# MLP up in a hybrid encoder layer: each matmul as two over half of the contraction, summed by ScalarE and VectorE

## The chip, the cores and the metric

The kernel runs on one core of a Trainium2 chip. The metric is the device time of one execution in microseconds, as the median of several runs. The engines in the text: PE (TensorE) multiplies matrices and writes only to PSUM, an accumulator memory of 8 banks, each of 128 partitions by 512 fp32 values; PEld is its loading of weights; ACT (ScalarE) and DVE (VectorE) work elementwise; POOL is GpSimd; SP issues the DMAs that bring weights from main memory.

## The reference

One layer of an encoder over 512 tokens of 1024 features: a mixer with three branches, a cross-attention into 256 memory tokens, and a gated MLP, each between two RMS norms and with a residual. The change concerns the first half of the MLP:

```
D_MODEL = 1024; SEQ = 512; D_FF = 2816

def dwconv3(x, w):                      # centred, width 3, over the tokens, one filter per channel
    xp = jnp.pad(x, ((0, 0), (1, 1), (0, 0)))
    return xp[:, :-2] * w[0] + xp[:, 1:-1] * w[1] + xp[:, 2:] * w[2]

def conv_glu_ffn(h, w_up, w_conv, w_down):
    u = dwconv3(h @ w_up, w_conv)       # 512 x 5632
    g, val = jnp.split(u, 2, axis=-1)
    return (jax.nn.gelu(g, approximate=True) * val) @ w_down
```

All arrays are fp32.

## The kernel before

**Products in three parts.** Every fp32 operand is split into a high part (what the fp32r format holds; ACT makes it, `high`, line 75) and a low part (the rest; DVE makes it, `low`, line 78). A product is then three fp32r matmuls into one PSUM bank: high × high, high × low, low × high (`mm3`, lines 88 to 90). Weights come by DMA as blocks of 128 × 1024 (`wr`, three buffers), and are split into `wh` and `wl` (four buffers each), so a block's buffers come free when PE has finished the block four before.

**MLP up.** `mlp_up` makes the 5632 columns of `h @ w_up` as 44 blocks of 128 channels by 512 tokens, in the order gate 0, value 0, gate 1, value 1, and so on. A block takes 8 steps over the contraction (1024 = 8 × 128) of 3 matmuls, all into one bank (`mm`, four buffers in turn): the weights are 128 × 128 pieces of `wh` and `wl`, the moving operand is the normed input, `hh` and `hl`, with 512 columns. The first four blocks (`AHEAD`) are made in two halves of 256 tokens each, because the last two of the four token tiles are still being normed; the other 40 are made whole, by `project_all`.

**What follows a block.** `conv3` does the convolution out of PSUM in three steps into an SBUF tile `u`: ACT writes the middle tap (line 322), DVE adds the left tap (323) and the right tap (331), each reading the bank again. Then ACT applies `gelu` to a gate block (line 1021); for a value block DVE multiplies by the gate (1024), ACT makes the high part of the result and DVE the low part (75 and 78, both called `act`), which stay in SBUF for MLP down.

**MLP down.** `mlp_down` takes four `mm` banks, one for each tile of 128 tokens, and accumulates over 22 `act` tiles, twice (for the two halves of the 1024 output columns).

**What sets the order.** A scheduler places the instructions of each engine in one list ahead of time, and on the chip each engine works through its list in order, waiting on semaphores where an operand or a buffer isn't ready. In the middle of MLP up the scheduler puts, for each block n, the splitting of the weights of block n+4 ahead of block n's convolution, on ACT and on DVE. Banks and buffers go round: block n+4 writes the bank of block n. `aux` names a second set of four PSUM banks, used by transposes, attention and sums elsewhere, and by nothing in MLP up before the change.

Of the kernel before, what the change touches and what calls it, by code (L numbers as in the profile page):

```python
# [9 lines left out]
ALU = mybir.AluOpType  # L10
# [3 lines left out]
P = 128  # L14
# [3 lines left out]
KD = D // P  # L18
# [32 lines left out]
class Trunk:  # L51
# [865 lines left out]
    def project_all(self, ps, w, ht):  # L917
        for k in range(KD):
            c = slice(k * P, (k + 1) * P)
            self.mm3(ps[:], tuple(q[:, c] for q in w), tuple(q[:, :, k, :] for q in ht), k == 0, k == KD - 1)  # L920


    def keys(self, kv, mem, tiles):
        km = []
        for kt in tiles:
            ps = self.project(self.d["xa_wk"][kt], mem, M)
            h, lo = (kv.tile([P, M], F32R, tag="km" + q, bufs=KD, name="km") for q in "hl")
            self.split(h[:], lo[:], ps[:, :M])
            km.append((h[:], lo[:]))
        return km  # L930
# [65 lines left out]
    def mlp_up(self, tp, ap, ht, last):  # L996
        nc, d = self.nc, self.d
        order = [i + KF * s for i in range(KF) for s in range(2)]
        pend = []
        for n, c in enumerate(order[: self.AHEAD]):  # L1000
            w = self.block(d["ffn_up"][c])
            ps = self.mm_bank()
            self.project_half(ps, w, ht, 0)
            pend.append((w, ps))
            if n == 1:
                last[0]()
        last[1]()
        act = []
        for n, c in enumerate(order):
            if n < self.AHEAD:  # L1010
                w, ps = pend[n]
                self.project_half(ps, w, ht, 1)
            else:
                w = self.block(d["ffn_up"][c])
                ps = self.mm_bank()
                self.project_all(ps, w, ht)
            val = n % 2
            u = tp.tile([P, L], F32, tag="u%d" % val, bufs=2, name="u")
            self.conv3(u[:], ps[:], [FFW + tap * 44 + c for tap in range(3)])
            if not val:  # L1020
                nc.scalar.activation(out=u[:], in_=u[:], func=ACT.Gelu_apprx_tanh)
                g = u
            else:
                nc.vector.tensor_tensor(out=u[:], in0=u[:], in1=g[:], op=ALU.mult)  # L1024
                h, lo = (ap.tile([P, L], F32R, tag="act" + q, bufs=KF, name="act") for q in "hl")
                self.split(h[:], lo[:], u[:])
                act.append((h, lo))
        return act
# [319 lines left out]
```

## Time and profile before

| | us |
|---|---|
| median of 3 runs | 1096.74 (1094.62 to 1097.0) |
| the profiled execution | 1093.87 |
| its span, first to last instruction | 1092.1 |
| last matmul of the half-made blocks; first of the whole ones | 747.38; 747.50 |
| last matmul of MLP up; first of MLP down | 964.91; 965.13 |
| first matmul of MLP down into its fourth bank | 969.02 |

How to read it: times in the profile are microseconds from the start of the span. A row of the order of time has the start, the duration, the engine, the line of the kernel, the instruction, what it writes and reads by the program's names, and the shapes; in brackets stands how long the engine had been idle and what ended that. A row of the waits has who waited for whom, the sum, the count and the longest. A row of a group has the count, then busy time, mean ns of one, and idle time ahead. A row of a stretch has its length, then busy time (and count) of PE, PEld, DVE, ACT and POOL, and PE's granted clock (1.00 is full).

### The profile page before, as it was taken

To read this page: it belongs to the slowest core of one execution; us is meant where nothing else is said; L and a number is where in the kernel's file an instruction comes from. 1 tells how busy PE (TensorE), PEld (TensorE's weight loads), DVE (VectorE), ACT (ScalarE), POOL (GpSimd) and SP (SyncE) were. 2 spreads that over 40 slices of the span, in tenths; PEclk is the share of its full clock that TensorE was granted. 3 is DMA by queue.
4 is the path that set the end of the run, shared out by engine and by line. 5 is a ranking of instruction groups with operands and counts; after the bars stand their busy time and mean duration, and the time that the engine had idled before them with its cause. 6 is when DMAs were issued, how large, how long until landed. Compare 5 with 4: busy or idle time off the path is not lost.

```text
span 1092.1 us, 13531 instructions
## 1 busy us (share of the span) xinstructions
PE 1071.0 (98%) x5232; PEld 895.3 (82%) x5232; DVE 691.7 (63%) x1037; ACT 476.8 (44%) x744; POOL 66.2 (6%) x56
## 2 busy tenths in 40 slices
PE   8889999999999999999999999999999999999997
PEld 6677888887888888888798888898888888888886
DVE  6898799986665763436795456577565656542324
ACT  6554443326557642324564445345444444431211
POOL 0161120001110100000000000000000000000000
PEclk9889999999999999999999999999999999999999
DMA  6354622326332322226245321133222222222212
GB/s 222 106 192 159 234 100 97 129 84 178 110 117 93 104 78 97 97 96 230 98 151 196 117 77 53 64 98 116 97 97 97 97 97 97 97 97 97 97 58 77
DMA packets 43532, 125.48 MB, mean 115 GB/s; under 512 B 5097, under 2 KB 11561, under 8 KB 43468
## 3 DMA queue, kind: packets, MB, share of 16 engines
q1 hardware_dynamic: 43468, 124.62, 33.5%
q8 instruction: 41, 0.67, 0.2%
q14 instruction: 23, 0.19, 0.0%
HBM read 115.16 MB, written 7.34 MB: 112 GB/s over the span
## 4 chain that ended last, share of the span: by engine, by line
PE 88%; DVE 5%; DMA 4%; ACT 2%; issue 1%; SPq 1%; DVEq 0%; ACTq 0%
PE mm L88 26%; PE mm L89 26%; PE mm L90 26%; PE aux L89 2%; PE aux L88 2%; PE aux L90 2%; DMA wr<-in_w_out 1%; DVE wl L78 1%; DMA wr<-in_w_in 1%; PE aux L725 1%; PE aux L714 1%; PE aux L904 1%; DMA raw<-in_hy_f 1%; ACT wh L75 1%; DMA v<-vd 0%
## 5 line engine op out<-in xcount | busy, mean ns | idle before, releaser
L78 DVE TENSOR_TENSOR wl<-wr,wh 128x1024 fp32r<-128x1024 f32 (+1 forms) x171 | 216.8, 1270 | 250.9 <-ACT wh L75 248.1
L75 ACT ACTIVATE wh<-wr 128x1024 fp32r<-128x1024 f32 (+1 forms) x171 | 180.1, 1054 | 304.1 <-PE mm L89 177.4
L89 PE MATMUL mm<-hl,wh 128*128 128x512 f32 (+1 forms) x448 | 167.5, 374 | 0.0
L88 PE MATMUL mm<-hh,wh 128*128 128x512 f32 (+1 forms) x448 | 167.2, 374 | 0.2 <-ACT hh L75 0.2
L90 PE MATMUL mm<-hh,wl 128*128 128x512 f32 (+1 forms) x448 | 167.4, 374 | 0.0
L88 PE MATMUL mm<-xh,wh 128*128 128x512 f32 x416 | 164.0, 394 | 0.0
L89 PE MATMUL mm<-xl,wh 128*128 128x512 f32 x416 | 163.2, 392 | 0.0
L90 PE MATMUL mm<-xh,wl 128*128 128x512 f32 x416 | 162.6, 391 | 0.0
L90 PEld LDWEIGHTS mm<-hh,wl 128*128 128x128 f32 x448 | 84.3, 188 | 15.0
L88 PEld LDWEIGHTS mm<-hh,wh 128*128 128x128 f32 x448 | 84.1, 188 | 15.3 <-ACT hh L75 0.5
L89 PEld LDWEIGHTS mm<-hl,wh 128*128 128x128 f32 x448 | 84.4, 188 | 15.0 <-DVE hl L78 0.2
L88 PEld LDWEIGHTS mm<-xh,wh 128*128 128x128 f32 x416 | 78.6, 189 | 16.2 <-issue 0.3
L90 PEld LDWEIGHTS mm<-xh,wl 128*128 128x128 f32 x416 | 78.4, 188 | 16.4
L89 PEld LDWEIGHTS mm<-xl,wh 128*128 128x128 f32 x416 | 78.5, 189 | 15.8 <-issue 0.3
L88 PE MATMUL mm<-wh,act 128*128 128x512 f32 x176 | 68.5, 389 | 0.0
L89 PE MATMUL mm<-wl,act 128*128 128x512 f32 x176 | 68.5, 389 | 0.0
L90 PE MATMUL mm<-wh,act 128*128 128x512 f32 x176 | 68.3, 389 | 0.0
L75 ACT ACTIVATE act<-u 128x512 fp32r<-128x512 f32 x22 | 13.9, 631 | 57.8 <-DVE u L1024 57.8
L88 PEld LDWEIGHTS mm<-wh,act 128*128 128x128 f32 x176 | 33.0, 188 | 7.1 <-issue 0.3
L90 PEld LDWEIGHTS mm<-wh,act 128*128 128x128 f32 x176 | 33.0, 188 | 6.9
L89 PEld LDWEIGHTS mm<-wl,act 128*128 128x128 f32 x176 | 33.0, 188 | 6.8
L331 DVE SCALAR_TENSOR_TENSOR u<-mm,cols,u 128x511 f32<-128x511 f32 x44 | 33.1, 751 | 1.5
(338 smaller groups left out, 1895.9 us busy)
## 6 DMA issues: line engine op xcount, KB each, us to landing
wr<-in_w_in SPq DMA_DIRECT2D x55, 512.0 KB, 3.5
wr<-in_ffn_up SPq DMA_DIRECT2D x44, 512.0 KB, 3.5
wr<-in_ffn_down SPq DMA_DIRECT2D x22, 512.0 KB, 3.4
wr<-in_w_branch SPq DMA_DIRECT2D x12, 512.0 KB, 3.4
kd<-kt SPq DMA_DIRECT2D x16, 256.0 KB, 3.8
kst<-kd SPq DMA_DIRECT2D x8, 512.0 KB, 4.9
wr<-in_w_out SPq DMA_DIRECT2D x8, 512.0 KB, 4.0
wr<-in_xa_wk SPq DMA_DIRECT2D x8, 512.0 KB, 3.4
```

What stands on the lines that cost most here:

```text
L75: self.nc.scalar.activation(out=out, in_=in_, func=ACT.Copy, bias=0.0, scale=scale)
L78: (eng or self.nc.vector).tensor_tensor(out=out, in0=in_, in1=f(high), op=ALU.subtract)
L88: mm(out, ah, bh, start=first, stop=False)
L89: mm(out, ah, bl, start=False, stop=False)
L90: mm(out, al, bh, start=False, stop=last)
L331: nc.vector.scalar_tensor_tensor(out=out[:, 0 : L - 1], in0=ps[:, 1:L], scalar=self.colvec(w2), in1=out[:, 0 : L - 1], op0=ALU.mult, op1=A ...
L714: nc.tensor.transpose(tr[:, i * P : (i + 1) * P], s[:, i // 2, (i % 2) * P : (i % 2 + 1) * P], self.ident[:])
L725: self.nc.tensor.matmul(po[64 * e : 64 * e + 64, b * P : (b + 1) * P], v[b, j][:, (h + e) * 64 : (h + e + 1) * 64], pt[:, (2 * i + j) * P ...
L904: self.nc.tensor.transpose(tr[:, k * P : (k + 1) * P], t[:, c : c + P], self.ident[:])
```

## The change

Of the 40 whole blocks, each matmul over 128 rows of the contraction is made as two over 64 rows each: rows 0 to 63 into an `mm` bank, rows 64 to 127 into an `aux` bank, in turns. The two matmuls of a pair use the two halves of the array's rows. After the block, ACT copies the `aux` bank into the tile `u`, DVE adds `u` to the `mm` bank in place, and the convolution reads the `mm` bank as before. The first four blocks stay as they were. Lines after these move by 14 (the multiplication by the gate is at 1038 then, `gelu` at 1035); the new add is line 1032.

```
@@ -919,6 +919,16 @@
+    def project_rows(self, banks, w, ht):
+
+        mm = self.nc.tensor.matmul
+        for k in range(KD):
+            c = slice(k * P, (k + 1) * P)
+            (wh, wl), (xh, xl) = (q[:, c] for q in w), (q[:, :, k, :] for q in ht)
+            for i, (a, b) in enumerate(((wh, xh), (wh, xl), (wl, xh))):
+                for ps, r in zip(banks, (slice(0, 64), slice(64, P))):
+                    mm(ps[:], a[r], b[r], start=k == i == 0, stop=k == KD - 1 and i == 2)
@@ -1012,10 +1022,14 @@
             else:
                 w = self.block(d["ffn_up"][c])
-                ps = self.mm_bank()
-                self.project_all(ps, w, ht)
+                banks = self.mm_bank(), self.aux_bank()
+                self.project_rows(banks, w, ht)
+                ps, other = banks
             val = n % 2
             u = tp.tile([P, L], F32, tag="u%d" % val, bufs=2, name="u")
+            if n >= self.AHEAD:
+                self.high(u[:], other[:])
+                nc.vector.tensor_tensor(out=ps[:], in0=ps[:], in1=u[:], op=ALU.add)
             self.conv3(u[:], ps[:], [FFW + tap * 44 + c for tap in range(3)])
```

The order on ACT for a pair of blocks late in MLP up, before (`wh` is the split of the block four later, `u_…<-mm_…` the middle tap, the third row `gelu`):

```order
L75 ACTIVATE wh_8184<-wr_8186 128x1024
L322 ACTIVATE u_8063<-mm_8038,cols_176 128x512
L1021 ACTIVATE u_8063<-u_8063 128x512
L75 ACTIVATE wh_8220<-wr_8222 128x1024
L322 ACTIVATE u_8099<-mm_8074,cols_176 128x512
L75 ACTIVATE act_8104<-u_8099 128x512
L75 ACTIVATE wh_8283<-wr_8285 128x1024
```

and the same place on ACT after the change:

```order
L75 ACTIVATE wh_9210<-wr_9212 128x1024
L75 ACTIVATE u_9006<-aux_8957 128x512
L322 ACTIVATE u_9006<-mm_8956,cols_176 128x512
L1035 ACTIVATE u_9006<-u_9006 128x512
L75 ACTIVATE wh_9273<-wr_9275 128x1024
L75 ACTIVATE u_9069<-aux_9020 128x512
L322 ACTIVATE u_9069<-mm_9019,cols_176 128x512
L75 ACTIVATE act_9076<-u_9069 128x512
L75 ACTIVATE wh_9363<-wr_9365 128x1024
```

The copy of the `aux` bank has come between the split of the weights and the middle tap; the rest keeps its place. On DVE, the same pair of blocks before:

```order
L78 TENSOR_TENSOR wl_8221<-wr_8222,wh_8220 128x1024
L323 SCALAR_TENSOR_TENSOR u_8099<-mm_8074,cols_176,u_8099 128x511
L331 SCALAR_TENSOR_TENSOR u_8099<-mm_8074,cols_176,u_8099 128x511
L1024 TENSOR_TENSOR u_8099<-u_8099,u_8063 128x512
L78 TENSOR_TENSOR act_8105<-u_8099,act_8104 128x512
L78 TENSOR_TENSOR wl_8284<-wr_8285,wh_8283 128x1024
```

and after:

```order
L78 TENSOR_TENSOR wl_9274<-wr_9275,wh_9273 128x1024
L1032 TENSOR_TENSOR mm_9019<-mm_9019,u_9069 128x512
L323 SCALAR_TENSOR_TENSOR u_9069<-mm_9019,cols_176,u_9069 128x511
L331 SCALAR_TENSOR_TENSOR u_9069<-mm_9019,cols_176,u_9069 128x511
L1038 TENSOR_TENSOR u_9069<-u_9069,u_9006 128x512
L78 TENSOR_TENSOR act_9077<-u_9069,act_9076 128x512
L78 TENSOR_TENSOR wl_9364<-wr_9365,wh_9363 128x1024
```

The add stands behind the split of the weights and ahead of the two side taps. On PE, where MLP down begins, the scheduler puts off the fourth bank (the one that the last block of MLP up has used) while it fills the first three. Before, 17 matmuls stand ahead of the first row of this piece that writes `mm_8282`:

```order
L89 MATMUL mm_8281<-wl_8284,act_6736 128x512
L88 MATMUL mm_8282<-wh_8283,act_6674 128x512
L89 MATMUL mm_8282<-wl_8284,act_6674 128x512
L90 MATMUL mm_8282<-wh_8283,act_6675 128x512
L90 MATMUL mm_8281<-wh_8283,act_6737 128x512
```

and 22 ahead of the first that writes `mm_9362` now:

```order
L90 MATMUL mm_9359<-wh_9393,act_6867 128x512
L88 MATMUL mm_9360<-wh_9393,act_6866 128x512
L88 MATMUL mm_9362<-wh_9363,act_6674 128x512
L89 MATMUL mm_9362<-wl_9364,act_6674 128x512
L90 MATMUL mm_9362<-wh_9363,act_6675 128x512
```

The fourth bank comes five matmuls later, behind four of the next weight block.

## The prediction

> **What bounds the kernel now.** I read the page's busy shares first, then the stretch of the changed stage by itself, then who waits for whom in it, then its order of time.
>
> ```profile
> PE 1071.0 (98%) x5232; PEld 895.3 (82%) x5232; DVE 691.7 (63%) x1037; ACT 476.8 (44%) x744; POOL 66.2 (6%) x56
> ...
> 747.50:964.90 217.40, 217.40 (x961) 180.01 (x960) 135.14 (x163) 91.34 (x122) 0.00 (x0) 1.00 0.28 100
> ...
> 747.50 0.40 PE L88 MATMUL mm<-hh,wh 128*128 128x512 f32 x1
> ...
> 964.91 0.39 PE L90 MATMUL mm<-hh,wl 128*128 128x512 f32 x1
> 965.13 0.39 PE L88 MATMUL mm<-wh,act 128*128 128x512 f32 x1
> ```
>
> The second row is the stretch of the 40 whole MLP-up blocks: PE (third number) is busy for all 217.40 us at full clock, DVE for 62% and ACT for 42%. Its 960 matmuls start from 747.50 to 964.91, so one follows another by 217.41/959 = 0.2267 us (each record is longer, since they overlap), and a block of 24 takes 5.44 us. PE sets the pace. Busy shares alone would say that ACT and DVE have ample room. They don't, because they work in turns. The waits of the same stretch, and its order of time over two blocks (start, duration; in brackets the idle time and what ended it):
>
> ```profile
> DVE wl L78 <- ACT wh L75: 65.4, 39, 2.8
> ACT act L75 <- DVE u L1024: 54.9, 19, 2.9
> ACT u L1021 <- DVE u L331: 45.1, 21, 2.3
> ACT wh L75 <- PE mm L89: 25.3, 39, 2.5
> ...
> 763.83 1.06 ACT L75 ACTIVATE wh<-wr 128x1024 fp32r<-128x1024 f32 x1 [0.28 <-PE mm L89]
> 764.79 0.67 ACT L322 ACTIVATE u<-mm,cols 128x512 f32<-128x512 f32 x1
> 767.69 0.63 ACT L1021 ACTIVATE u<-u 128x512 f32<-128x512 f32 x1 [2.22 <-DVE u L331]
> 769.26 1.06 ACT L75 ACTIVATE wh<-wr 128x1024 fp32r<-128x1024 f32 x1 [0.95 <-PE mm L89]
> 770.23 0.67 ACT L322 ACTIVATE u<-mm,cols 128x512 f32<-128x512 f32 x1
> 773.79 0.63 ACT L75 ACTIVATE act<-u 128x512 fp32r<-128x512 f32 x1 [2.89 <-DVE u L1024]
> 774.71 1.06 ACT L75 ACTIVATE wh<-wr 128x1024 fp32r<-128x1024 f32 x1 [0.28 <-PE mm L89]
> ...
> 764.92 1.23 DVE L78 TENSOR_TENSOR wl<-wr,wh 128x1024 fp32r<-128x1024 f32 x1 [0.65 <-ACT wh L75]
> 766.06 0.74 DVE L323 SCALAR_TENSOR_TENSOR u<-mm,cols,u 128x511 f32<-128x511 f32 x1
> 766.84 0.75 DVE L331 SCALAR_TENSOR_TENSOR u<-mm,cols,u 128x511 f32<-128x511 f32 x1
> 770.36 1.23 DVE L78 TENSOR_TENSOR wl<-wr,wh 128x1024 fp32r<-128x1024 f32 x1 [2.77 <-ACT wh L75]
> 771.50 0.74 DVE L323 SCALAR_TENSOR_TENSOR u<-mm,cols,u 128x511 f32<-128x511 f32 x1
> 772.28 0.75 DVE L331 SCALAR_TENSOR_TENSOR u<-mm,cols,u 128x511 f32<-128x511 f32 x1
> 773.07 0.69 DVE L1024 TENSOR_TENSOR u<-u 128x512 f32<-128x512 f32 x1
> ```
>
> ACT waits only for DVE, except that its `wh` waits for PE; `wh` stands in ACT's queue behind the previous block's last step. So there is a loop ACT → DVE → ACT once per block. Count it from `wh` until ACT can take the next `wh` (an ACT instruction starts some 0.10 us before the one ahead ends: 763.83 + 1.06 against 764.79). Even block (a gate half, ends with `gelu`): 767.69 + 0.63 − 0.10 − 763.83 = 4.39 us. Odd block (a value half, ends with `act`): 773.79 + 0.63 − 0.10 − 769.26 = 5.06 us. A pair takes the loop 9.45 us and PE 2 × 5.44 = 10.88. The 1.43 us that are left are the idle times 0.28 and 0.95, and a bit at the seams. **That is the real margin of this stage: 0.7 us per block.**
>
> **The change, part by part.**
>
> *1. The matmuls.* 960 become 1920, each over 64 rows, in pairs on different rows of the array. This trace has no such pair. Its nearest rows are the attention's pairs on different columns (64 of them each), beside whole-width ones of the same 128-column, plain-fp32 kind:
>
> ```profile
> 287.30 1.10 PE L725 MATMUL aux<-npt,v 128*64 128x128 f32 x16
> ...
> 703.84 1.03 PE L904 MATMUL aux<-ident,nt 128*128 128x128 f32 x8
> ...
> L725 PE MATMUL aux<-npt,v x128: 272/273/324, 287.3 to 396.5; 128*64 128x128 f32 x128
> ```
>
> Whole ones follow each other by (1.03 − 0.27)/7 = 0.109 us, half ones by (1.10 − 0.27)/15 = 0.055: a pair on two halves of the array costs one whole matmul, weight loads included. The bounds of the new pair are thus 0.227 us (fully side by side) and 2 × 0.227 = 0.454 (one after the other). I take 0.227, the row of the same sort of pair: 0 us. It matters little where in the lower part it falls: PE decides again only above 6.2 us per block (below), 0.258 us per pair.
>
> The Trainium skill (TensorE: Matmul & The Clock Gate, section "Part 3: Packing small matmuls — row/col tiling") has row tiles run side by side too, but gives 3.07 times for four of them, not four. By that yield (77%) a pair would cost an estimated 0.295 us and the stage +66 us; the column pairs above show no such loss.
>
> *2. Two instructions per block, and where they stand.* ACT copies the second bank to `u`; DVE adds it to the first bank in place; only then can ACT's middle tap read the sum. Nearest rows for the copy and the add:
>
> ```profile
> L75 ACT ACTIVATE fly<-aux 128x512 f32<-128x512 f32 x8 | 4.6, 592 | 1.0 <-PE aux L90 0.8
> L281 DVE TENSOR_TENSOR scaled<-mm,scale 128x512 f32<-128x512 f32 x3 | 1.9, 675 | 0.0
> L782 DVE TENSOR_TENSOR gsum<-mm,gsum 128x512 f32<-128x512 f32 x8 | 5.5, 690 | 5.5 <-PE mm L90 5.5
> L341 DVE TENSOR_SCALAR hfa<-aux,hysmall 128x512 f32<-128x512 f32 x1 | 0.8, 796 | 0.0
> ```
>
> Copy 0.59, add 0.69; no row writes PSUM from DVE, so the add lies between 0.675 and 0.80. In the order, DVE has `wl` of block n+4, then the add of block n, then the two side taps; ACT has `wh` of n+4, copy, tap, `gelu` or `act`. Counted from `wh`: the copy runs 0.97 to 1.56, beside `wl` (1.09 to 2.32), so it costs nothing. The add starts where the first side tap stood, at 2.24, and ends at 2.93. The middle tap, until now hidden beside `wl` (764.79 to 765.46), comes after it: a hop DVE to ACT (0.10 at 767.69, 0.03 at 773.79; I take 0.07), 0.67 us, a hop back (764.92 − 764.89 = 0.03; I take 0.04): 3.71. The first side tap so moves from 2.24 to 3.71: **+1.47 us per block** (0.69 + 0.67 + 0.11), and all behind it with it. The loop is then 5.86 (even) and 6.53 (odd), 12.39 per pair, against PE's 10.88. The loop becomes the bound, by 1.51 us per pair.
>
> *3. From when to when.* ACT and DVE are in step with PE at the first whole block, whose matmuls end at 752.94 (`wh` waits for that); before it stands the `act` of the last half-made block, so I let the loop start at 753.5:
>
> ```profile
> 752.25 0.69 DVE L1024 TENSOR_TENSOR u<-u 128x512 f32<-128x512 f32 x1
> ...
> 752.95 1.06 ACT L75 ACTIVATE wh<-wr 128x1024 fp32r<-128x1024 f32 x1 [2.53 <-PE mm L89]
> ...
> 968.12 0.75 DVE L331 SCALAR_TENSOR_TENSOR u<-mm,cols,u 128x511 f32<-128x511 f32 x1
> ...
> 968.53 0.39 PE L88 MATMUL mm<-wh,act 128*128 128x512 f32 x1
> 968.76 0.39 PE L89 MATMUL mm<-wl,act 128*128 128x512 f32 x1
> 969.02 0.47 PE L88 MATMUL mm<-wh,act 128*128 128x512 f32 x1
> ```
>
> 39 loops (20 even, 19 odd) take 117.2 + 124.1 = 241.3 us; in the 40th the second side tap ends at 3.02 + 1.47 + 0.75 = 5.24. It frees the last block's bank at 753.5 + 241.3 + 5.2 = 1000.0, where before it was 968.87, and the matmul of MLP-down that takes this bank started at 969.02. So 31.1 us later. By then PE has done 22 matmuls of MLP-down instead of 17 (the order shows it), which saves 5 × 0.227 = 1.1. **Sum: +30.0 us.**
>
> PE doesn't feel it at once. A block needs the bank of the block four before it; at first the loop frees it some 10.5 us early (second side tap of the fifth block at 753.5 + 5.2 = 758.7, wanted at 747.50 + 4 × 5.44 = 769.3), and loses 0.76 per block, so PE runs freely for about 14 blocks more and waits 0.75 us per block from about 845 us on (some 16 us in all); the last 14 or so it pays ahead of MLP-down, waiting bank by bank, some 5 us at a time. Weights aren't late: `wh` is split four blocks ahead. DVE then is busy for 135.1 + 27.6 us and ACT for 91.3 + 23.7, in a stretch of some 250.
>
> The Trainium skill (same page, "Part 1: The HAM clock gate") says that PE falls to half its clock after an idle window of some 3.4 us. By that the matmuls between these last waits would run slower, an estimated 1 to 2 us more; no row here shows it.
>
> The profiled execution took 1093.87 us, so 1123.9 now; the median of the runs shown lies 2.9 above it, and I forecast **1127**.
>
> **The rivals.**
>
> *Halves one after the other.* The pair costs 0.454 us, a block 10.9: PE hides the loop, and 960 × 0.227 = 218 us come on top: 1315. For it: no row shows two halves of the rows side by side, and then the change doesn't do what it says. Against: the column pairs.
>
> *Partly side by side.* If the two weight loads of a pair must follow each other at their full length,
>
> ```profile
> L88 PEld LDWEIGHTS mm<-hh,wh 128*128 128x128 f32 x448 | 84.1, 188 | 15.3 <-ACT hh L75 0.5
> ```
>
> a pair costs 2 × 0.188 = 0.376, a block 9.0, and the time grows by 960 × 0.149 = 143 us to 1240; any price between 0.258 and this falls between. Against: 256-column matmuls with such loads follow by 0.12 (rows below), so loads overlap.
>
> *Not slower.* The pair gets cheaper than the whole, and ACT and DVE keep up:
>
> ```profile
> 747.14 0.28 PE L88 MATMUL mm<-hh,wh 128*128 128x256 f32 x1
> 747.26 0.28 PE L89 MATMUL mm<-hl,wh 128*128 128x256 f32 x1
> 747.38 0.28 PE L90 MATMUL mm<-hh,wl 128*128 128x256 f32 x1
> ```
>
> 256 columns cost 0.12 and 512 cost 0.227, so some 0.013 of each matmul is not columns; were that hidden under the other half, 960 × 0.013 = 12.5 us would go: 1084. It decides only where the loop stays under 24 × 0.214 = 5.1 us per block. For that the add and the tap would have to cost 0.4 us, not 1.47.
>
> **How the numbers follow.** Loop-bound 0.82; one after the other 0.09; partly 0.05; not slower 0.04. In the likeliest case the add's bounds give −0.6 to +4.2 us (40 × −0.015 to 0.106), hops of 0.03 or 0.10 each −2.0 to +3.6, and the start of the loop and the waits ahead of MLP-down a few more either way; with the runs' own spread I take 1114 to 1148. That leaves out the other three cases, 0.18. What this measurement can tell from no change is about 0.2%: faster 0.03, same 0.01, slower 0.96.
>
> **What would show it.** Right: pairs of `mm` and `aux` matmuls at 0.227 us or little more per pair; PE waiting for DVE's L331, from the middle of the stage; ACT's L322 waiting for the new DVE add for some 1.4 us per block, DVE's L323 waiting for ACT's L322 for 0.7 to 0.8; a loop of 12.4 us per pair of blocks; MLP-up some 16 us longer, and the rest as waits in MLP-down's first 25 matmuls. Wrong: PE busy through the whole stage with pairs of over 0.258 us, or ACT's `wh` still waiting for PE late in the stage.

## The result, and the profile after

The change makes the kernel slower: a median of 1125.67 us (1122.69 to 1127.46) beside 1095.68 us (1094.02 to 1097.0) of the kernel before on the same chip. The ratio is 1.0261, with a 95% interval of 1.0231 to 1.0291. The forecast was 1127.

The page's busy shares after, and the stretch of MLP up cut in three (length, then busy time and count of PE, PEld, DVE, ACT and POOL, PE's granted clock, share and rate of DMA):

```profile
PE 1080.0 (96%) x6192; PEld 913.2 (81%) x6192; DVE 718.4 (64%) x1077; ACT 496.1 (44%) x784; POOL 66.1 (6%) x56
...
747.50:845.00 97.50, 97.50 (x861) 80.90 (x861) 66.04 (x84) 45.47 (x66) 0.00 (x0) 1.00 0.29 93
845.00:985.00 140.00, 130.62 (x1089) 119.01 (x1085) 90.65 (x113) 62.69 (x91) 0.00 (x0) 1.00 0.27 87
985.00:1005.00 20.00, 10.64 (x33) 7.93 (x34) 13.21 (x17) 8.55 (x13) 0.00 (x0) 0.66 0.27 79
```

The page alone hides it: PE's share fell by two points and DVE's rose by one. The stretches show it. Until 845 PE is busy all the time, as before. From then on it has gaps, and in the last 20 us it is busy for little more than half, at a granted clock of 0.66. DVE and ACT are far from full in each stretch, so it isn't their amount of work that PE waits for.

Who waits for whom from 747.5 to 1003 (sum, count, longest):

```profile
ACT u L322 <- DVE mm L1032: 56.7, 40, 1.4
...
DVE u L323 <- ACT u L322: 30.3, 40, 0.8
...
PE mm L88 <- DVE u L331: 10.5, 3, 4.9
PE mm L930 <- DVE u L331: 7.4, 10, 0.7
```

Two waits are new, each once in all 40 blocks: ACT's middle tap for the add (L1032), 1.42 us a time, and DVE's side tap for the middle tap, 0.76 us. ACT's `wh` is no longer in the list as waiting for PE: now PE waits, for DVE's right tap (L331), which frees the banks. ACT's and DVE's order of time over a pair of blocks:

```profile
793.01 1.04 ACT L75 ACTIVATE wh<-wr 128x1024 fp32r<-128x1024 f32 x1
793.96 0.58 ACT L75 ACTIVATE u<-aux 128x512 f32<-128x512 f32 x1
795.95 0.69 ACT L322 ACTIVATE u<-mm,cols 128x512 f32<-128x512 f32 x1 [1.42 <-DVE mm L1032]
798.30 0.63 ACT L1035 ACTIVATE u<-u 128x512 f32<-128x512 f32 x1 [1.66 <-DVE u L331]
798.84 1.05 ACT L75 ACTIVATE wh<-wr 128x1024 fp32r<-128x1024 f32 x1
...
805.34 1.04 ACT L75 ACTIVATE wh<-wr 128x1024 fp32r<-128x1024 f32 x1
```

```profile
794.08 1.23 DVE L78 TENSOR_TENSOR wl<-wr,wh 128x1024 fp32r<-128x1024 f32 x1 [0.26 <-ACT wh L75]
795.22 0.69 DVE L1032 TENSOR_TENSOR mm<-mm,u 128x512 f32<-128x512 f32 x1
796.67 0.75 DVE L323 SCALAR_TENSOR_TENSOR u<-mm,cols,u 128x511 f32<-128x511 f32 x1 [0.76 <-ACT u L322]
797.46 0.75 DVE L331 SCALAR_TENSOR_TENSOR u<-mm,cols,u 128x511 f32<-128x511 f32 x1
```

ACT waits for nothing ahead of `wh`, so the distance from one `wh` to the next is the loop itself: 798.84 − 793.01 = 5.83 us for the even block and 805.34 − 798.84 = 6.50 for the odd one, 12.33 per pair, where PE needs 10.88.

PE's order of time: the pairs of half-height matmuls in the middle of the stage, then the end of MLP up and the start of MLP down.

```profile
750.08 0.50 PE L930 MATMUL mm<-hh,wh 64*128 64x512 f32 x1
...
800.08 0.39 PE L930 MATMUL mm<-hl,wh 64*128 64x512 f32 x1
800.08 0.39 PE L930 MATMUL aux<-hl,wh 64*128 64x512 f32 x1
800.30 0.39 PE L930 MATMUL mm<-hh,wl 64*128 64x512 f32 x1
...
800.53 0.39 PE L930 MATMUL mm<-hh,wh 64*128 64x512 f32 x1
...
853.82 0.47 PE L930 MATMUL mm<-hh,wh 64*128 64x512 f32 x1
...
860.32 0.46 PE L930 MATMUL mm<-hh,wh 64*128 64x512 f32 x1 [0.74 <-DVE u L331]
...
982.50 0.39 PE L930 MATMUL aux<-hh,wl 64*128 64x512 f32 x1
...
989.49 0.77 PE L88 MATMUL mm<-wh,act 128*128 128x512 f32 x1 [4.90 <-DVE u L331]
990.05 0.63 PE L89 MATMUL mm<-wl,act 128*128 128x512 f32 x1
990.48 0.63 PE L90 MATMUL mm<-wh,act 128*128 128x512 f32 x1
995.98 0.77 PE L88 MATMUL mm<-wh,act 128*128 128x512 f32 x1 [4.87 <-DVE u L331]
...
1001.48 0.79 PE L88 MATMUL mm<-wh,act 128*128 128x512 f32 x2
```

Both matmuls of a pair start together, and pairs follow each other by 0.225 us on these rows, as whole matmuls did. Until PE has to wait, a block starts every 5.44 us, from the second at 755.65 to the nineteenth at 848.13: PE itself lost nothing. The twentieth is the first that starts late, at 853.82, 0.42 us behind the pair ahead of it; from there blocks start 6.50 and 5.83 us apart, by turns. The list of waits has only 7.4 us of this, because a record is longer than the distance to the next one, so a late start shows as idle time only in part. MLP down then waits twice for almost 5 us, and the second matmul of the last row is the first into the fourth bank, at about 1001.8 (the row's end, 1002.27, less the 0.47 us of such a first matmul).

In this execution everything was late by 2.6 us before the changed code began: the first pair starts at 750.08, the first whole matmul before at 747.50. This start differs from one profiled execution to the next, with pairs (747.53 to 753.87 in the runs below) as with whole matmuls (749.30 and 753.45 in two of them). Less those 2.6 us, the last matmul of MLP up (982.50 against 964.91) is 15.0 us later and the fourth bank (1001.8 against 969.02) 30.2 us later. So half of the loss is inside the stage and half at the four banks ahead of MLP down.

### The profile page after: what moved, and what is told of

It reads as the page before. It is cut to its first block, busy times and chain, and to the rows that moved or that the text cites. A ratio compares the mean times of both kernels' runs of the same rounds, so it can differ in the third digit from the quotient of the medians.

```text
span 1123.7 us, 15531 instructions
## 1 busy us (share of the span) xinstructions
PE 1080.0 (96%) x6192; PEld 913.2 (81%) x6192; DVE 718.4 (64%) x1077; ACT 496.1 (44%) x784; POOL 66.1 (6%) x56
## 4 chain that ended last, share of the span: by engine, by line
PE 74%; DVE 14%; ACT 6%; issue 3%; DMA 3%; SPq 0%; POOL 0%; DVEq 0%; ACTq 0%; POOLq 0%
PE mm L88 19%; PE mm L89 19%; PE mm L90 19%; PE mm L930 8%; DVE wl L78 4%; ACT wh L75 3%; DVE u L323 2%; DVE u L331 2%; PE aux L89 2%; PE aux L88 2%; PE aux L90 2%; ACT u L322 2%; DVE mm L1032 1%; PE aux L725 1%; DVE u L1038 1%
## 5 line engine op out<-in xcount | busy, mean ns | idle before, releaser
L930 PE MATMUL mm<-hh,wh 64*128 64x512 f32 x320 | 125.5, 392 | 8.2 <-DVE u L331 7.4
L930 PE MATMUL aux<-hh,wh 64*128 64x512 f32 x320 | 126.3, 395 | 0.0
L930 PE MATMUL aux<-hh,wl 64*128 64x512 f32 x320 | 123.8, 387 | 0.0
L930 PE MATMUL mm<-hl,wh 64*128 64x512 f32 x320 | 123.7, 387 | 0.0
L930 PE MATMUL aux<-hl,wh 64*128 64x512 f32 x320 | 123.7, 386 | 0.0
L930 PE MATMUL mm<-hh,wl 64*128 64x512 f32 x320 | 123.6, 386 | 0.0
L88 PE MATMUL mm<-wh,act 128*128 128x512 f32 x176 | 70.0, 398 | 10.5 <-DVE u L331 10.5
L930 PEld LDWEIGHTS mm<-hh,wh 64*128 64x128 f32 x320 | 58.9, 184 | 22.8 <-issue 16.5
L930 PEld LDWEIGHTS mm<-hh,wl 64*128 64x128 f32 x320 | 58.9, 184 | 6.2
L930 PEld LDWEIGHTS mm<-hl,wh 64*128 64x128 f32 x320 | 58.9, 184 | 6.2
L930 PEld LDWEIGHTS aux<-hl,wh 64*128 64x128 f32 x320 | 59.0, 184 | 0.1
```

Of the source, the lines that this page charges most:

```text
L88: mm(out, ah, bh, start=first, stop=False)
L930: mm(ps[:], a[r], b[r], start=k == i == 0, stop=k == KD - 1 and i == 2)
```

## The experiments

The theory: a pair costs what a whole matmul costs, and the whole loss is the loop on ACT and DVE, lengthened by the add and by the middle tap behind it. The rivals: the half-height matmuls cost something themselves, or the new instructions cost by the mere amount of work on the two engines.

**The pairs without the sum.** The changed kernel without the copy and the add:

```
-            if n >= self.AHEAD:
-                self.high(u[:], other[:])
-                nc.vector.tensor_tensor(out=ps[:], in0=ps[:], in1=u[:], op=ALU.add)
```

> The changed kernel with its pairs of half-height matmuls, but without the copy and the add: the second bank is never read, so half of the contraction is left out of MLP up. Theory (ACT and DVE taking turns set the pace, and the turn is 1.47 us per block too long through the add): the turn is the old one again, 9.45 us per pair of blocks, below PE's 10.88, so PE sets the pace and the time is that of the kernel before, 1096 within 3 us. Rival 1 (the pairs themselves cost the time on PE): it stays at 1126. Rival 2 (the copies and adds load ACT, DVE or PSUM, wherever they stand): 1096 too, so this run tells only rival 1 apart.

Measured: 1098.28 us (1096.18 to 1103.64), ratio 1.0032 (1.0013 to 1.005). That is between 1.4 and 5.5 us over the kernel before (2.3 by the medians); the rest of the loss of 30 is gone with the sum. Its first and last pair:

```profile
753.87 0.50 PE L930 MATMUL mm<-hh,wh 64*128 64x512 f32 x1
...
971.38 0.39 PE L930 MATMUL mm<-hh,wl 64*128 64x512 f32 x1
```

From one to the other it is 217.51 us, where whole matmuls took 217.41. So in the changed stage the pairs cost 0.1 us. The profiled execution (1100.56 us) is 6.7 us over the one before, and 6.4 of them are there before its first pair starts; why the ten executions are 2.3 us longer in the median stays open.

**The sum without the pairs, in the same turn.** Whole matmuls into one bank again, but with the two instructions of the sum where the change has them: ACT copies the bank to `u`, DVE takes the larger of bank and `u` in place (which is the bank). The splits of the weights are held in the changed kernel's order, ahead of the block's copy:

```
+            if n + 4 < len(order):
+                with ExitStack() as behind:
+                    for i in ends:                       # last steps of the block before
+                        behind.enter_context(self.tc.issue_after(i.ins))
+                    ahead.append(self.block(d["ffn_up"][order[n + 4]]))
...
+                with self.tc.issue_after(made[0].ins), self.tc.issue_after(made[1].ins):
+                    self.high(u[:], ps[:])
+                    nc.vector.tensor_tensor(out=ps[:], in0=ps[:], in1=u[:], op=ALU.max)
```

> The kernel before, with whole-height matmuls, but with a copy of the block's own bank by ACT and, in place of the add, a maximum of the bank and the copy by DVE (which leaves the values as they are), at the places where the changed kernel has its copy and its add (behind the splits of the weights of block n+4, ahead of the middle tap). Theory: the turn becomes 12.3 to 12.4 us per pair of blocks without any half-height matmul, and the time 1126 within 5 us (the last four blocks aren't held in this order, which may give back 2 or 3 us). Rival 1 (the pairs cost the time): 1096. Rival 2 (load, wherever it stands): 1126.

Measured: 1112.46 us (1109.63 to 1115.46), ratio 1.0153 (1.0127 to 1.0178). The direction is the theory's, the size about half. ACT's order of time in this kernel, in the middle of the stage and at its end:

```profile
789.81 1.04 ACT L75 ACTIVATE wh<-wr 128x1024 fp32r<-128x1024 f32 x1
...
796.32 1.04 ACT L75 ACTIVATE wh<-wr 128x1024 fp32r<-128x1024 f32 x1
...
802.15 1.05 ACT L75 ACTIVATE wh<-wr 128x1024 fp32r<-128x1024 f32 x1
...
975.78 1.55 ACT L75 ACTIVATE u<-mm 128x512 f32<-128x512 f32 x3
...
978.17 1.85 ACT L321 ACTIVATE u<-mm,cols 128x512 f32<-128x512 f32 x3
```

The loop is the same to 0.01 us: 796.32 − 789.81 = 6.51 and 802.15 − 796.32 = 5.83. But the last four blocks, whose order the edit didn't hold, are done in batches: three copies in a row, then three taps. That gives back the lag that the loop had built up, and with it the half of the loss ahead of MLP down. The expectation had put this freedom at 2 or 3 us; it was 13.

**The last four blocks alone.** To test that half directly: the changed kernel with only the splits of MLP down's first four weight blocks moved, behind the taps of the last four blocks of MLP up.

```
-                ws.append(self.block(d["ffn_down"][n, kp]))
+                ws.append(self.block(d["ffn_down"][n, kp]) if n or kp > 3 else self.block_behind(40 + kp, d["ffn_down"][n, kp]))
...
+    def block_behind(self, n, src):                      # split behind the taps of block n
+        tap, side = self.taps[n]
+        with self.tc.issue_after(tap.ins), self.tc.issue_after(side.ins):
+            return self.block(src)
```

> The changed kernel with the splits of the first four weight blocks of MLP down alone put behind the taps of the last four blocks of MLP up (on ScalarE behind the middle tap, on VectorE behind the last side tap); the order of all blocks ahead of them is the changed kernel's. Theory: about half of the 30 us is lost ahead of MLP down, where PE waits some 5 us at a time for banks that the loop on ScalarE and VectorE frees late; the last four blocks then go through 1.5 us (the first) and on the mean some 1 us each (the others: 10.2 us per pair of blocks instead of 12.3) faster, the last bank is free 4 to 5 us earlier, the waits of 4.9 us get shorter by that much in all, and the time is 1118 to 1122 us. Rival: the waits ahead of MLP down are not the loop's (the weights of MLP down would be as late); then the time stays at 1125 to 1128 us.

Measured: 1121.16 us (1120.0 to 1123.05), ratio 1.024 (1.0225 to 1.0254). The time is the theory's, though this interval and the changed kernel's overlap; the trace says more. DVE's last right tap, and PE's waits of MLP down:

```profile
995.56 0.75 DVE L331 SCALAR_TENSOR_TENSOR u<-mm,cols,u 128x511 f32<-128x511 f32 x1
...
PE mm L88 <- DVE u L331: 7.5, 2, 5.1
PE mm L930 <- DVE u L331: 7.5, 10, 0.8
```

The last bank is free at 996.31, where the changed kernel's own last right tap ends at 1001.66 (its row stands further down): 5.35 us earlier. PE's waits ahead of MLP down fall from 10.5 us to 7.5, while those inside MLP up stay as they were (7.4 and 7.5). The waits at the banks are the loop's. Not all of the 5.35 us reaches the end. PE, at a slower clock behind its wait of 5.1 us (0.43 us per matmul, more on this below), comes to that bank only at 997.05, 4.75 us earlier than in the changed kernel, and by then has done 17 matmuls of MLP down, not 22, which takes back 1.1. The 3.6 us that are left are about what the profiled executions differ by (1125.60 and 1122.22).

**The sum without the pairs, in the scheduler's order.** The kernel before with the same copy and maximum as in the second experiment, but with no order held; the scheduler then puts the splits behind the taps.

```
+            if n >= self.AHEAD:
+                self.high(u[:], ps[:])
+                nc.vector.tensor_tensor(out=ps[:], in0=ps[:], in1=u[:], op=ALU.max)
```

> As the run with whole-height matmuls, copy and maximum, but with the order left to the scheduler, which here puts the splits of the weights behind the middle tap and the right tap by itself. Same instructions as that run. Theory: 1096 to 1099, since the turn is then about 10.5 us per pair of blocks. Rival 2 (the added work costs its time wherever it stands): 1126, as the other.

Measured: 1095.72 us, ratio 1.0002 (0.9987 to 1.0018). The same two instructions per block cost nothing in another place of the lists. In this trace ACT's `wh` stands behind the middle tap and waits for PE, and from one `wh` to that of the next pair of blocks it is 803.70 − 792.82 = 10.88 us, PE's own time again.

**The change itself, with the splits behind.** The changed kernel, pairs and sum as they are; only the splits of block n+4 are held behind block n's taps (the middle one on ACT, the right one on DVE), for MLP down's first four as well:

```
-                w = self.block(d["ffn_up"][c])
+                w = self.block_behind(n - 4, d["ffn_up"][c])
```

> The changed kernel with one order turned: the splits of the weights of block n+4 stand behind block n's taps, on ACT behind the middle tap and on DVE behind the right tap, and not ahead of its copy and add. All instructions are the same. Theory: the middle tap no longer waits for an add that waits for the low part of the weights; counted from add to add on DVE an even block takes about 4.3 us and an odd one 6.2, 10.5 per pair of blocks against PE's 10.88, so PE sets the pace again and the time is 1096 to 1099. Rival 1 (pairs) and rival 2 (load of the added work on ACT, DVE and PSUM, wherever it stands): 1126.

Measured: 1096.69 us (1096.14 to 1100.23), ratio 1.0012 (1.0002 to 1.0022). All of the loss is gone but for some 0.7 us by the medians (0.2 to 2.4 by the interval), with the same instructions on every engine. ACT's order of time, and the late stretch as far as the last matmul of MLP up stood before:

```profile
795.29 1.05 ACT L75 ACTIVATE wh<-wr 128x1024 fp32r<-128x1024 f32 x1
...
804.22 0.60 ACT L75 ACTIVATE u<-aux 128x512 f32<-128x512 f32 x1 [0.50 <-PE aux L930]
...
806.17 1.05 ACT L75 ACTIVATE wh<-wr 128x1024 fp32r<-128x1024 f32 x1
```

```profile
845.00:964.90 119.90, 119.90 (x1060) 99.09 (x1060) 86.77 (x111) 62.11 (x89) 0.00 (x0) 1.00 0.32 97
```

From `wh` to `wh` of the next pair it is 806.17 − 795.29 = 10.88 us, PE's own time for two blocks. PE is busy through the late stretch (119.90 of 119.90 us), and the copy now waits for PE (0.50). The split, 1.0 us on ACT and 1.1 on DVE, fills the time in which each engine would wait for the other; in the changed kernel's order it stood ahead of the sum, and each step of the block came after it.

**A second add in the loop.** The changed kernel with another add on DVE, of zeros to the same bank, behind the first:

```
+                nc.vector.tensor_tensor(out=ps[:], in0=ps[:], in1=zero, op=ALU.add)
```

> The changed kernel with a second add per block behind the first, of a tile of zeros into the same bank, ahead of the middle tap. Theory: it lies in the turn, which grows by 0.72 us per block (0.69 and a seam), so 40 x 0.72 = 29 us more than the changed kernel: 1154. Rival 2 (what counts is how busy DVE is, and DVE is busy for 64% of the span): much less than that, since DVE still has idle time.

Measured: 1157.76 us (1156.65 to 1158.86), ratio 1.0573 (1.0543 to 1.0604), some 32 us over the changed kernel, where the theory had 29. The first row of this kernel's waits from 747.5 to 1003 (35 of the 40 blocks; the rest come later here):

```profile
ACT u L322 <- DVE mm L1036: 77.5, 35, 2.2
```

ACT's wait for the sum is 77.5 / 35 = 2.21 us on the mean, longer by 0.79 than the 56.7 / 40 = 1.42 of the changed kernel: the add and the step to it, for which the theory had 0.72. Times 40 that is 31.6 us, nearly the whole of the difference: in the loop each block's lengthening goes to the end undiminished.

**The same add aside.** The same number of elements added into a spare tile on DVE, behind the right tap, where nothing reads it:

```
+                with self.tc.issue_after(side.ins):
+                    nc.vector.tensor_tensor(out=junk, in0=zero, in1=zero, op=ALU.add)
```

> The changed kernel with the same additional add per block on DVE, 0.69 us, but of zeros into a spare tile, behind the right tap, where DVE then waits 1.7 us for ACT's split of the next weights (even blocks), or ahead of the multiplication by the gate (odd blocks). Theory: even blocks pay nothing, odd blocks pay it in full, since their multiplication and ACT's act stand behind it: 20 x 0.72 = 14 us more than the changed kernel, 1140. Rival 2 (load on DVE): the same as the run with the add in the turn, whatever that is.

Measured: 1136.07 us (1132.68 to 1136.6), ratio 1.0369 (1.0336 to 1.0401), some 10 us over the changed kernel. ACT's `wh` to `wh` in its order of time:

```profile
797.72 1.04 ACT L75 ACTIVATE wh<-wr 128x1024 fp32r<-128x1024 f32 x1
...
804.70 1.04 ACT L75 ACTIVATE wh<-wr 128x1024 fp32r<-128x1024 f32 x1
```

The odd block takes 6.98 us, 0.48 more; 20 of them make 9.6 us. In the even block the add lies beside `gelu` and costs nothing. The theory had the odd blocks pay the whole 0.72, some 14 us in all. They pay less, since this add, which uses nothing of the tap ahead of it, starts 0.67 us after the right tap (802.18 and 802.85), and the multiplication 0.60 us after it (803.45), together 1.27, where the multiplication alone, which does need the tap, starts 0.79 us after it (in the changed kernel 988.59 and 989.38). So the same add on the same engine costs 32 us in one place and 10 in another: the place decides, not the amount of work.

**The halves in threes, in sixes and in sequence.** The last three runs ask what "in turns" is worth. The list of matmuls has three of one half, then three of the other:

```
-            for i, (a, b) in enumerate(((wh, xh), (wh, xl), (wl, xh))):
-                for ps, r in zip(banks, (slice(0, 64), slice(64, P))):
+            for ps, r in zip(banks, (slice(0, 64), slice(64, P))):
+                for i, (a, b) in enumerate(((wh, xh), (wh, xl), (wl, xh))):
```

> The changed kernel with another order of each six half-height matmuls: three on the lower rows, then three on the upper ones, in place of turns. Theory (matmuls start in order, and one starts beside the one ahead only if it uses other rows): of six, only the fourth starts beside the third, and the next step's first beside the sixth, so a step takes four times 0.227 us in place of three, or five or six if a change of rows isn't free; a block takes 8 x 4 x 0.227 = 7.26 us, more than the turn of ACT and DVE (6.2), and PE sets the pace: 40 x (7.26 - 5.44) = 73 us above the kernel before, 1168. If PE could pull a later matmul ahead of a waiting one, 1126; if the halves never ran side by side, 1314.

Measured: 1126.12 us (1124.32 to 1129.54), ratio 1.0287 (1.0246 to 1.0328). Nothing is lost, against the likelier expectation: pairs still follow by 0.227 us.

The same in groups of six, and with all 24 of a block's one half ahead of all 24 of the other (in both, the two inner loops go over groups of `steps`, 6 or 24 long):

```
+        steps = [(k, i) for k in range(KD) for i in range(3)]
+        for g in range(0, 24, 6):                        # 24 for the halves in sequence
+            for ps, r in zip(banks, (slice(0, 64), slice(64, P))):
+                for k, i in steps[g : g + 6]:
```

> The changed kernel with the twenty-four half-height matmuls of each half taken in turns of six (two k steps of the upper rows, then two of the lower rows) instead of one by one; the same matmuls, sums and banks. Theory: a matmul over the other half of the rows starts as soon as its own rows are free, ahead of matmuls in the list that wait for theirs, by a few instructions at most; the list in threes gave 1126 us, so three can be overtaken. If six can be overtaken as well: 1126 us and pairs at 0.227 us. Rival: the reach is about four instructions; then in each group of six two or three run without a partner, a pair takes some 0.30 to 0.34 us on the mean, the 40 blocks of MLP up take about 24 x 0.08 to 0.11 = 2 to 2.7 us more each, of which the loop on VectorE hides 0.7, and the time is 1180 to 1210 us.

> The changed kernel with all twenty-four matmuls of the upper rows first and then all twenty-four of the lower rows, for each block, instead of in turns; the same matmuls, sums and banks. Theory: only what stands close in the list can run side by side; then nearly every half-height matmul takes the 0.227 us of a whole one by itself, a block takes 10.9 us instead of 5.4, and the time is 1290 to 1320 us (40 x 5.44 = 218 us over the kernel before's 1096, less the few that overlap where the halves meet). Rival: PE finds the other half's matmuls at any distance: 1126 us.

Measured: 1125.56 us for the sixes (ratio 1.029, 1.0251 to 1.0329) and 1254.15 us (1252.54 to 1257.16) in sequence, ratio 1.1453 (1.1422 to 1.1485). PE's order of time in the latter, around the place where the list passes from the upper half (`mm`) to the lower half (`aux`) of a block:

```profile
800.60 0.39 PE L932 MATMUL mm<-hh,wl 64*128 64x512 f32 x1
800.61 0.49 PE L932 MATMUL aux<-hh,wh 64*128 64x512 f32 x1
800.82 0.39 PE L932 MATMUL mm<-hh,wh 64*128 64x512 f32 x1
...
801.05 0.39 PE L932 MATMUL mm<-hl,wh 64*128 64x512 f32 x1
...
801.28 0.39 PE L932 MATMUL mm<-hh,wl 64*128 64x512 f32 x1
801.40 0.39 PE L932 MATMUL aux<-hh,wh 64*128 64x512 f32 x1
...
805.29 0.49 PE L932 MATMUL mm<-hh,wh 64*128 64x512 f32 x1
```

The time is well below the 1290 to 1320 us expected. The first `aux` matmul starts at 800.61, ahead of three `mm` matmuls that stand before it in the list (800.82, 801.05, 801.28). After that the `aux` ones run alone at 0.23 us each until 805.29, where the next block's first overtakes in the same way. One half takes 805.29 − 800.61 = 4.68 us instead of 24 × 0.227 = 5.44, a block 9.36. That is 3.92 us over the 5.44 of a block of whole matmuls; times 40, 157 us over the kernel before, 1252.7 by this count and 1254.15 measured. So here a matmul on the other half of the rows starts three matmuls early, and no more. The expectation for the sixes had reckoned that such a reach (it put it at about four) would leave two or three of each group alone. The start of the stage in the run with sixes shows why it doesn't:

```profile
748.14 0.50 PE L932 MATMUL mm<-hh,wh 64*128 64x512 f32 x1
...
748.72 0.49 PE L932 MATMUL aux<-hh,wh 64*128 64x512 f32 x1
748.94 0.39 PE L932 MATMUL mm<-hh,wh 64*128 64x512 f32 x1
```

Of the first six `mm` matmuls three run alone (748.14, 748.48, 748.71). Then the first `aux` matmul starts at 748.72, again ahead of three `mm` ones that stand before it in the list (748.94, 749.17, 749.40). From there the two halves run side by side, with `mm` ahead: the seventh `mm` matmul starts at 749.63, before the last two of the six `aux` ones ahead of it in the list (749.76 and 749.98). It stays so: matmuls of the same place in the two halves start 0.68 us apart, which is three of 0.227, and a block takes 5.44 us until PE has to wait for its banks. So a reach of three is enough for groups of six.

The kernel's description says that each engine works through its list in order. For PE's matmuls on two halves of the rows these runs show that this holds only up to those three.

The Trainium skill (TensorE: Matmul & The Clock Gate, section "Part 3: Packing small matmuls — row/col tiling") says that matmuls start and end strictly in the order of the program, with no reordering. The starts in the rows above differ, for two halves of the array's rows: three matmuls are overtaken.

## Why the prediction was right, by its own steps

**1. The matmuls: 0 us. Right.** Pairs follow at 0.227 us, and without the sum the 40 blocks take 217.51 us, for 217.41 before. That kernel as a whole, at 1098.3 us, is at most 0.5% slower (the interval's end), which isn't the 66 us that the Trainium skill's yield for four tiles (TensorE: Matmul & The Clock Gate, the same section) would have made. The rivals "one after the other" and "partly side by side" fall with it. The halves in sequence show what the first would have looked like.

**2. The loop: +1.47 us per block. Right to 0.03.** In the changed kernel the copy is hidden beside `wl`, as said (793.96 to 794.54, `wl` until 795.31), and the first side tap starts 796.67 − 793.01 = 3.66 us after `wh`, for a forecast of 3.71. The add took 0.69, within its bounds of 0.675 to 0.80; the hop behind it was 0.04 instead of 0.07. The loop was 5.83 and 6.50 (forecast 5.86 and 6.53).

**3. From when to when: +30.0 us. Right, with its parts within 1 us once the late start is taken off.** ACT and DVE at the two ends of the loop in the changed kernel:

```profile
755.99 1.04 ACT L75 ACTIVATE wh<-wr 128x1024 fp32r<-128x1024 f32 x1
```

```profile
1000.91 0.75 DVE L331 SCALAR_TENSOR_TENSOR u<-mm,cols,u 128x511 f32<-128x511 f32 x1
```

The loop starts at 755.99, 2.5 us after the 753.5 of the forecast: this is the late arrival of 2.6 us, not the change. It frees the last bank at 1001.66 (1000.91 + 0.75), so the 39 loops and the last taps took 245.7 us where the forecast had 246.5. MLP up got 15.0 us longer (forecast some 16), and the rest came as waits of 4.90 and 4.87 us ahead of MLP down, as said. The point from which PE waits was put a block too early: 845 (847.6 with the late start), and the first block that starts late is the one at 853.82. The loop loses 0.73 us per block against PE, not 0.76, so PE's lead of 10.6 us lasts for 14.6 blocks and not 14, and the next whole block is the first to wait. This moves a little of the loss from the stage to the banks and doesn't change the sum.

The forecast's last step added 2.9 us, by which the profiled execution of before lay below its median. After, the profiled execution took 1125.6 us, its own median: so the 2.6 us of late arrival belong to the spread between executions that this step stood for, and the medians differ by 30.0 us, the sum. That they agree to the decimal is luck: the loops and last taps are 0.8 us shorter than the sum has them, and the two profiled executions, less the late arrival, differ by 29.2.

**The clock.** PE falls to a slower clock after its idle time: behind the wait of 4.90 us, matmuls follow by 990.48 − 990.05 = 0.43 us instead of 0.227, at a granted clock of 0.66 in that stretch. This agrees with the rule of the Trainium skill (TensorE: Matmul & The Clock Gate, section "Part 1: The HAM clock gate"), by which the forecast had named an estimated 1 to 2 us more. The slow matmuls are there, but the trace shows no time that they add: the ones behind the last wait are done when the fourth bank comes free (1001.66, its first matmul at 1001.8), so at full clock PE would have waited for that bank instead. That was close: in the run with the last four blocks changed, the bank is free at 996.31 and PE comes to it at 997.05, so there the slow matmuls do add some 0.6 us (0.74 less the 0.15 from a bank's being free to its first matmul).

**"Not slower" and its condition.** That rival decided only if add and tap were to cost 0.4 us in the loop. They cost 1.44 there; but with the splits behind, the time is 1096.69, so the change can indeed be all but free, by a way that the prediction had not priced: the same instructions in another order. Nor did the pair get cheaper than the whole: that would have been 1084, and the pairs alone gave 1098.28.

## What to carry to other kernels

Where two engines work in turns, an added step costs what it adds to one turn, times the number of turns, less the margin to the engine that sets the pace; busy shares of 62% and 42% said nothing of that. Before giving up such a change, look what stands between the steps of the turn: independent work (here the split of the next weights) belongs into the time in which the engines wait for each other, and moving it there recovered all but about 1 of the 30 us. When the loop runs slower than the engine it feeds, part of the loss shows only where the buffers run out, here at the start of the next stage.

## What the runs showed of the hardware

- Two fp32r matmuls of 64 rows, on the two halves of the array's rows and into two banks, start together and take 0.227 us per pair, what one matmul of 128 rows takes.
- They need not stand side by side in the list: turns of three and of six run as fast as turns of one (1126.12 and 1125.56 us, for 1125.67). ACT and DVE hold up all three kernels, but the traces too have pairs at 0.227 us. A matmul overtakes up to three of the other half that stand before it in the list (748.72 and 800.61 in the rows above); with 24 of each, the rest runs alone (1254.15 us).
- A DVE add of 512 fp32 columns from PSUM and SBUF back into the same bank takes 0.69 us, no more than one that writes to SBUF (0.675 and 0.69 in the forecast's rows).
- After 4.9 us without work, PE's matmuls follow by 0.43 us instead of 0.227 (granted clock 0.66 over the 20 us around them).
